# Running the FFN output of one sequence inside the attention stage of the next

## The chip, the cores and the metric

The kernel runs on all 8 cores of one Trainium2 chip. Each core computes 4 of the 32 sequences on its own; no core waits for another. The time is device microseconds (us) of the slowest core. The kernels have a second, slower state in some executions: the cores of one die, or of both, show a lower granted TensorE clock, and the time is 1% to 17% longer.

## The reference, cut to what matters

```python
h = rms_norm(x, g_pre_mix)
proj = h @ w_in                                    # 1024 -> 4352
o_a = stick_breaking_attention(q_a, k_a, v_a)      # 8 heads x 64, strictly causal
o_b = dilated windows, 3 groups x 4 heads x 64, rotary q/k, merged by denominators
o_c = softmax(q_c @ k_mem) @ v_mem                 # 4 heads x 128, 256 memory tokens
merged = sum(sigmoid(h @ w_gate + b)[j] * (o_j @ w_br_j) for j in (a, b, c))
x = x + rms_norm(merged @ w_o, g_post_mix)
h2 = rms_norm(x, g_pre_ffn)
f = (silu(h2 @ w_gate_ffn) * (h2 @ w_up)) @ w_ffn_out      # 1024 -> 2816 -> 1024
x = x + rms_norm(f, g_post_ffn)
```

x has the shape (32, 2048, 1024), in float32; the matmuls are bf16.

## The kernel before: the parts that matter

A recorder takes every operation with what it reads and writes. A list scheduler then walks through them with estimated durations and fixes the order on each engine, before anything runs. Operations belong to lanes; a lane spreads its operations over a range of virtual time, and the scheduler takes the ready one with the least virtual time. An operation that opens an accumulator also needs a free PSUM bank, out of the banks that its tile allows.

```python
LAT = {"pe": 230, "act": 130, "dve": 110, "pool": 130, "sp": 100}   # ns until another engine sees a result, as the plan estimates it
...
ALLB = tuple(range(8))
YB = (5, 6, 7)            # projections of both lanes, everything of the dilated and memory lane
# stick-breaking scores use the pairs (0,1) and (2,3), its output bank 4
...
for s in range(nseq):
    a0 = 2.0 * s
    ...
    xo = lane(a0 - 0.002, 1.0, lambda: lane_X(s, lastFI), True)    # stick-breaking
    yo = lane(a0, 1.0, lambda: lane_Y(s, lastFI), True)            # memory, then dilated
    if s == 0:
        lane(a0 + 0.01, 0.0, conv)      # f32 -> bf16 copies of the dense weights, DRAM to DRAM, by GpSimd
    def beta():                         # the dense stage
        M1(0, [lastX, lastY])           # gates and branch projections of 512 tokens
        for c in range(4):
            lm = M2(s, c)                       # output projection, norm, residual
            if c > 0: lo = [FO(s, c - 1)]       # FFN output: 4 blocks x 44 matmuls of 512 columns
            if c < 3: M1(c + 1, [lm])
            res["fi"] = FI(c, lo)               # FFN input
            if nxt: P1(s + 1, c, (1,), ALLB, [res["fi"]])   # next sequence's norm and transposes
        FO(s, 3)
    lane(a0 + 1.0, 1.0, beta, True)
```

In the stick-breaking lane the causal mask of a diagonal block is a matmul that adds a constant to the scores:

```python
mms.append((scores of head e, Kb, Q[:, e, lo:512], True, False))
if j >= 0:
    mms.append((first 128 columns of them, ident, negmaskA, False, False))
```

The softmax here doesn't subtract the row's maximum and nothing guards it: scores larger than these inputs give would overflow.

## Time and profile before

| | before |
|---|---|
| fast runs | 5693.09 and 5689.79 us |
| slow runs | 5913.08 us, later 6471.97 |
| core spans in the profiled run (fast) | 5657.5 to 5685.4 us |
| matmuls | 31176 |

I use one account through the whole document. From the trace I take every matmul's start, and subtract from each start-to-start distance the streaming time of the first of the two: columns / 2.4 + 2.5 ns. The two constants fit this trace: they give 55.8, 109.2, 162.5 and 215.8 ns for 128, 256, 384 and 512 columns, where the commonest distances are 56, 109, 162 and 216 ns, and the dense runs of the profile show 215.8 ns for 512. What is left is time in which TensorE didn't stream. Each matmul belongs to a stage by its place in the fixed order. On the profiled core the streaming sums to 5220.1 us, so what isn't streaming is 456 us of 5676. By stage, as the mean of the six cores whose traces miss no matmul:

| not streaming, us | seq 1 | seq 2 | seq 3 | seq 4 |
|---|---|---|---|---|
| attention stage (the first with the start-up) | 135.8 | 78.1 | 79.0 | 78.1 |
| dense stage, with the seam before it | 21.7 | 19.8 | 17.2 | 13.1 |

So two kinds of hole exist: some 80 us in every attention stage, and a seam of about 20. The lines of the profile that carry this are in the prediction.

### The profile page before, as it was taken

The page shows a single profiled execution, that of the slowest core. Times are in us where ns is not written, and L with a number is a line of the kernel's source. Part 1 is how long each engine was busy: PE and PEld are TensorE (multiplying, and loading weights), DVE is VectorE, ACT ScalarE, POOL GpSimd, SP SyncE. Part 2 cuts the span into 40 slices and gives each one's busy share as a digit, 9 for nine tenths or more (in the row PEclk, how much of TensorE's full clock was granted, in tenths as well). Part 3 has the DMA queues.
Part 4 walks back from the last instruction along what each step waited for, and adds up shares of the span by engine and source line. Part 5 has one row for each costly group of instructions (what it writes and reads, how often), then busy time and mean ns, then how long its engine had stood idle before and what let it go on. Part 6 is the DMA issues. An engine that isn't in the chain of part 4 may idle for free.

```text
span 5685.4 us, 80515 instructions; the slowest of 8 cores (5657.5 to 5685.4 us)
## 1 busy us (share of the span) xinstructions
PE 5421.8 (95%) x31176; PEld 2701.1 (48%) x31176; DVE 2627.5 (46%) x3867; ACT 2827.9 (50%) x4063; POOL 546.9 (10%) x1185
## 2 busy tenths in 40 slices
PE   7998999999999989999999998999999999999999
PEld 4454444444445544444444554444444555444444
DVE  5455643333446654433344665443333556534332
ACT  6876732222588862222268785222227878522221
POOL 2111101001101110110111001011010101000000
PEclk9999999999999999999999999999999999999999
DMA  7553365545300125554531003555442101354443
GB/s 151 66 65 68 79 218 180 175 156 178 87 18 12 27 84 199 179 182 150 169 81 23 12 22 105 196 178 178 155 160 71 23 12 30 122 184 168 166 170 105
DMA packets 115646, 654.57 MB, mean 115 GB/s; under 512 B 13392, under 2 KB 13392, under 8 KB 65744
## 3 DMA queue, kind: packets, MB, share of 16 engines
q1 hardware_dynamic: 103760, 576.80, 29.6%
q0 software_dynamic: 11520, 72.62, 8.4%
q8 instruction: 263, 4.31, 0.3%
q14 instruction: 103, 0.84, 0.0%
HBM read 646.48 MB, written 95.42 MB: 130 GB/s over the span
## 4 chain that ended last, share of the span: by engine, by line
PE 84%; ACT 7%; DVE 3%; DMA 2%; issue 2%; POOL 2%; SPq 0%; POOLq 0%; ACTq 0%; DVEq 0%
PE ps L551 83%; ACT arena L567 7%; DVE arena L578 2%; DMA arena<-wallbf 1%; PE ps L560 1%; POOL arena L578 1%; DMA arena<-arena 1%; POOL arena L615 1%; DVE arena L583 1%; ACT arena L571 0%; POOL arena L613 0%; DMA arena<-x 0%; DVE arena L574 0%; DVE arena L586 0%; DVE arena L589 0%
## 5 line engine op out<-in xcount | busy, mean ns | idle before, releaser
L551 PE MATMUL ps<-arena 128*128 128x512 bf16 (+3 forms) x30088 | 5370.9, 338 | 195.5 <-ACT arena L567 80.9
L551 PEld LDWEIGHTS ps<-arena 128*128 128x128 bf16 x30088 | 2636.5, 101 | 2876.6 <-issue 474.8
L567 ACT ACTIVATE arena<-ps 128x1024 f32<-128x1024 f32 (+6 forms) x2336 | 1713.2, 769 | 1913.9 <-PE ps L551 1889.6
L578 DVE TENSOR_TENSOR arena<-arena 128x1024 bf16<-128x1024 bf16 (+7 forms) x1172 | 772.1, 661 | 368.5 <-ACT arena L567 343.3
L567 ACT ACTIVATE arena<-arena 128x1024 bf16<-128x1024 f32 (+4 forms) x904 | 805.2, 907 | 191.1 <-DVE arena L578 87.2
L578 DVE TENSOR_TENSOR arena<-arena,ps 128x512 bf16<-128x512 f32 (+1 forms) x480 | 380.2, 793 | 1004.8 <-PE ps L551 1004.2
L578 DVE TENSOR_TENSOR arena<-ps,arena 128x512 bf16<-128x512 f32 (+3 forms) x872 | 658.1, 770 | 268.5 <-PE ps L551 172.0
L567 ACT ACTIVATE arena<-ps,arena 128x512 f32<-128x512 f32 x384 | 263.1, 687 | 647.9 <-PE ps L551 647.2
L586 DVE SCALAR_TENSOR_TENSOR arena<-arena,ps 128x512 f32<-128x512 f32 x384 | 263.0, 687 | 444.0 <-PE ps L551 253.0
L574 DVE CAST arena<-ps 128x256 bf16<-128x256 f32 (+1 forms) x437 | 224.8, 515 | 324.7 <-PE ps L551 319.9
L586 DVE SCALAR_TENSOR_TENSOR arena<-ps,arena 128x1024 f32<-128x1024 f32 x128 | 164.1, 1282 | 374.4 <-POOL arena L615 374.0
L613 POOL TENSOR_SCALAR arena<-arena 128x1 f32<-128x1 f32 x264 | 71.6, 271 | 2501.9 <-ACT arena L567 2500.7
L578 POOL TENSOR_TENSOR arena<-arena 128x512 bf16<-128x512 bf16 (+3 forms) x172 | 179.1, 1042 | 648.1 <-ACT arena L567 591.1
L615 POOL TENSOR_TENSOR arena<-arena 128x1 f32<-128x1 f32 x264 | 158.3, 600 | 21.2
L560 PE MATMUL ps<-arena 128*128 128x128 bf16 x1088 | 86.1, 224 | 59.1 <-DVE arena L583 32.4
L583 DVE TENSOR_SCALAR arena<-arena 128x1024 bf16<-128x1024 f32 (+1 forms) x105 | 82.8, 789 | 81.4 <-POOL arena L615 78.1
L592 POOL DMA_DIRECT2D arena<-wall x52 | 29.7, 571 | 930.0 <-PE ps L551 928.3
L560 PEld LDWEIGHTS ps<-arena 128*128 128x128 bf16 x1088 | 70.1, 100 | 98.2 <-issue 82.5
L754 POOL COPY arena<-arena 128x256 bf16<-128x256 bf16 x115 | 51.2, 445 | 601.4 <-ACT arena L567 596.3
L571 ACT ACTIVATE arena<-ps 128x512 bf16<-128x512 f32 (+3 forms) x135 | 69.5, 515 | 49.3 <-PE ps L551 46.3
L583 DVE TENSOR_SCALAR arena<-ps 64x512 bf16<-64x512 f32 x96 | 65.9, 687 | 53.3 <-PE ps L551 50.6
L589 POOL MEMSET arena<- 128x1 f32 (+2 forms) x286 | 44.4, 180 | 369.7 <-PE ps L551 220.7
(13 smaller groups left out, 198.6 us busy)
## 6 DMA issues: line engine op xcount, KB each, us to landing
arena<-wallbf SPq DMA_DIRECT2D x208, 1024.0 KB, 4.9
arena<-wallbf SPq DMA_DIRECT2D x128, 1088.0 KB, 6.4
arena<-x SPq DMA_DIRECT2D x128, 512.0 KB, 5.8
out<-arena SPq DMA_DIRECT2D x128, 512.0 KB, 3.6
arena<-out SPq DMA_DIRECT2D x64, 512.0 KB, 4.9
arena<-wall POOLq DMA_DIRECT2D x40, 768.0 KB, 6.5
wallbf<-wall POOLq DMA_DIRECT2D x27, 1024.0 KB, 14.6
arena<-wallbf SPq DMA_DIRECT2D x4, 5632.0 KB, 23.3
```

The source lines that it names most:

```text
L551: return e.matmul(out(), lhsT=lhsT, rhs=rhs, start=start, stop=stop, skip_group_check=True)
L560: fns = [lambda e, o=o, i=i: e.transpose(o(), i, ident) for o, i in outs]
L567: return R.add([("act", cact(n), [lambda e: e.activation(out=lz(out), in_=lz(in_), func=func, **kw)])], r=r, w=w, fence=fence)
L571: return ("act", cact(n), [lambda e: e.activation(out=lz(out), in_=lz(in_), func=AF.Copy, **kw)])
L574: return ("dve", cdve(n, mode), [lambda e: e.tensor_copy(out=lz(out), in_=lz(in_))])
L578: return (eng, c, [lambda e: e.tensor_tensor(out=lz(out), in0=lz(in0), in1=lz(in1), op=op)])
L583: return (eng, c, [lambda e: e.tensor_scalar(out=lz(out), in0=lz(in0), scalar1=s1, scalar2=s2, op0=op0, **kw)])
L586: return ("dve", cdve(n, mode), [lambda e: e.scalar_tensor_tensor(out=lz(out), in0=lz(in0), scalar=s, in1=lz(in1), op0=op0, op1=op1)])
L589: return R.add([(eng, cpool(n) / 2 if eng == "pool" else cdve(n, "cp"), [lambda e: e.memset(ap, val)])], w=[ap])
L613: R.add([("pool", 200, [lambda e: e.tensor_scalar(out=v[:, 1:2], in0=v[:, 0:1], scalar1=1.0 / D, scalar2=eps, op0=ALU.mult, op1=ALU.add)]) ...
L615: R.add([("pool", 600, [lambda e: e.tensor_tensor(out=v[:, 2:3], in0=v[:, 1:2], in1=half, op=ALU.pow)])], r=[v[:, 1:2]], w=[v[:, 2:3]])
L754: ("pool", 500, [lambda e, o=sn[:, :, lo:lo + 128], i=SPt[:, :, lo:lo + 128]: e.tensor_copy(out=o, in_=i)])],
```

## The change

Intent: fill the holes of an attention stage with matmuls that don't depend on it. The FFN output of sequence s-1 is a long row of 512-wide matmuls that nothing in sequence s needs. For that the FFN activations (11.5 MB a sequence) go to DRAM and come back, SBUF is laid out anew, and the outputs of the three branches go through DRAM too. The order within a dense stage changes as well: the FFN input of 512 tokens now comes after the output projection of the next 512 (M2(c), FI(c-1), M1(c+1), where it was M2(c), M1(c+1), FI(c)). Besides, the mask becomes an add on VectorE, the rotary tables come in pieces as they are needed, weight buffers of the dense stage become four instead of three, and the weight conversion has four copies in flight instead of two (the scheduler's estimate of its rate goes from 150 to 130 bytes a ns).

```diff
 # what runs where
+def lane_F(s, banks, tbs, halves=(0, 1), load=True, after=()):
+    for h in halves:                      # half of the 1024 output columns at a time
+        ... load that half of w_ffn_out
+        for tb in tbs:                    # 128 tokens
+            T = Tile(banks)
+            ... load the activations from DRAM in two parts; 12 + 10 matmuls of 512
+            h == 0: square-sum, copy the raw half to DRAM;  h == 1: the norm of both halves, residual, store
-xo = lane(a0 - 0.002, 1.0, ...X)
-yo = lane(a0, 1.0, ...Y)
+xo = lane(a0 - 0.002, 1.0 * ..., ...X)
+yo = lane(a0, 0.9 * ..., ...Y)                        # the dilated lane ends earlier
+if s > 0:
+    f1: lane_F(s-1, YB, all 16 blocks, half 0); lane_F(s-1, YB, 12 blocks, half 1)
+    lane(a0 + 0.001, ..., f1)                         # filler inside attention
+    fo = lane(2*s + 1.0, 0.05, lane_F(s-1, ALLB, the last NF2 = 4 blocks, half 1))   # on the seam
 # dense stage of all but the last sequence: no FO
 # the mask
-mms.append((first 128 columns of the scores, ident, negmaskA, False, False))
+zd = both heads' first 128 columns in PSUM
+R.add([a_tt("dve", zd, zd, negmaskA for both heads, ALU.add, 256)])
 # branch outputs: two staging buffers a lane, then DRAM
-o = O[tc][:, 6 + h, :]
+o = A16(Y_OS + (u % 2) * 1024, 512)
+ospill(s, tc, 6 + h, o, f"yo{u % 2}")
 # FFN activations to DRAM, 512 pieces of 256 bytes a store, 88 stores a sequence
+DMA(ft_d[...][:, :, j, :], FT[:, j, :], ...)
 # stick-breaking projection weights: one buffer instead of two
-W = [A16(X_W[a], 3072) for a in range(2)]
+W = A16(X_W, 3072)
 # conversion
-... f"cv{k % 2}" ... if k < 2
+... f"cv{k % 4}" ... if k < 4
... (layout, last sequence, constants cut)
```

## The prediction

> **What bounds the kernel now.** I read the page's busy shares and its slices first, then the same 600 us of an attention stage and of a dense stage side by side, then the matmuls of both by width, then the chain that ended last where the two stages meet.
>
> ```profile
> span 5685.4 us, 80515 instructions; the slowest of 8 cores (5657.5 to 5685.4 us)
> PE 5421.8 (95%) x31176; PEld 2701.1 (48%) x31176; DVE 2627.5 (46%) x3867; ACT 2827.9 (50%) x4063; POOL 546.9 (10%) x1185
> ...
> PE   7998999999999989999999998999999999999999
> ...
> ACT  6876732222588862222268785222227878522221
> ```
>
> TensorE is busy nearly everywhere; ScalarE shows four attention stages (digits 5 to 8) and four dense stages (2). By busy time TensorE has only 5% left. That reading misleads, as the next two views show.
>
> ```profile
> 1500.00:2100.00 600.00, 568.16 (x3908) 310.13 (x3907) 334.87 (x572) 485.65 (x658) 56.71 (x75) 0.99 0.10 23
> 2200.00:2800.00 600.00, 593.33 (x2888) 273.78 (x2887) 229.25 (x279) 151.10 (x247) 50.43 (x148) 1.00 0.50 174
> ```
>
> Columns: PE, weight load, DVE, ACT and POOL busy, granted clock, DMA share, GB/s. First row: attention stage of the second sequence. Second: its dense stage. The matmuls of the two, by width:
>
> ```profile
> L551 PE MATMUL ps<-arena 128*128 128x512 bf16 x1759 | 420.3, 380 | 16.0 <-ACT arena L567 12.0 <-DVE arena L574 1.4 <-issue 0.5
> L551 PE MATMUL ps<-arena 128*128 128x128 bf16 x1740 | 145.8, 221 | 11.8 <-POOL arena L578 8.6 <-DVE arena L578 1.9 <-ACT arena L567 1.1
> L551 PE MATMUL ps<-arena 128*128 128x256 bf16 x293 | 73.7, 336 | 3.9 <-ACT arena L567 1.6 <-DVE arena L578 1.2 <-DVE arena L583 0.8
> L551 PE MATMUL ps<-arena 128*128 128x384 bf16 x116 | 32.9, 326 | 0.1
> ...
> L551 PE MATMUL ps<-arena 128*128 128x512 bf16 x2696 | 586.0, 379 | 0.0
> L560 PE MATMUL ps<-arena 128*128 128x128 bf16 x192 | 14.6, 219 | 6.7 <-ACT arena L571 6.7
> ```
>
> The first four rows are the attention stage, the last two the dense one. A row's mean of 380 ns is the length of one overlapped matmul, not its price. The price is in the chain, where a dense run stands alone:
>
> ```profile
> 2547.07 158.85 PE ps L551 x736
> ```
>
> 158.85/736 = 215.8 ns per 512 columns, 0.4215 ns a column. The attention rows hold 1759x512 + 1740x128 + 293x256 + 116x384 = 1,242,880 columns = 524 us of streaming in 600: 76 us are lost. The dense rows hold 1,404,928 columns = 592 us in 600: 8 us lost. So the kernel is bound by TensorE's stream, tightly in the dense stage (99%) and loosely in attention (87%). An attention stage is some 630 us long, so it loses about 80 us; in the first one I expect more. Where the stage ends, the chain shows the worst of it:
>
> ```profile
> 2092.10 1.05 PE ps L551 x5
> 2093.17 0.39 ACT arena L567
> ...
> 2093.63 0.68 POOL arena L578
> ...
> 2094.44 1.04 PE ps L551 x5
> ...
> 2104.26 10.53 PE ps L551 x48
> 2114.86 19.71 DMA arena<-wallbf
> ```
>
> The dilated lane runs alone there: five small matmuls, an exp, a mask on GpSimd, again five matmuls. From 2079.4 to 2104.3 the chain's TensorE pieces sum to 7.6 us, so about 17 us are waits, and then the first dense weights arrive late (TensorE is busy 34.3 of the 40 us from 2100 to 2140). In 2060 to 2100 the mean granted clock is 0.81.
>
> [...]
>
> **The change, part by part.**
>
> *Moved.* The FFN output of the first three sequences: 16 blocks x 44 matmuls of 512 = 704 x 215.8 ns = 152 us each. It leaves the dense stage and becomes a third lane of the next attention stage, except four half blocks (88 matmuls, 19 us) that are put on the seam where attention ends. The last sequence keeps it in its dense stage. No matmul is saved by this; what is gained is that it lies in the 80 us of holes. From the instruction order of the changed kernel, filler is some 15% of the matmul columns all along each later attention stage, in runs of one to eight matmuls, and the dilated lane now ends before the stick-breaking lane, so the tail shown above has filler and seam blocks in it.
>
> How much of a hole is filled I choose so, for one later stage: the tail and seam (about 23 us) shrink to 4; the start of the stage, about 10, to 6; the rest, about 47, splits into roughly 11 us in which 128-wide matmuls do not reach the streaming rate (estimate from the trace's start stamps), which filler cannot give back, and 36 us of short waits, of which I keep 13. Reason for keeping some: the order on TensorE is fixed before the run, so a wait on a matmul that comes later than the scheduler thought also holds up the filler behind it. Remaining 34 of 80, gain 46 us, times 3 = 138 us.
>
> *Removed.* Causal mask matmuls of the stick-breaking lane: 16 units x 4 diagonal blocks x 2 heads = 128 of width 128 per sequence, 128 x 128 x 0.4215 = 6.9 us; 4 sequences: 28 us of TensorE time. *Added* for it: 64 DVE adds of 256 columns in PSUM per sequence; the 256-column cast from PSUM takes 423 ns, so about 27 us of DVE, which has some 45% idle. On the lane's latency each adds half a microsecond or more between score and exp, hidden while other lanes have matmuls.
>
> *Added on other engines*, per later stage: 32 half-width squares at about 0.6 us and 16 copies at 0.7 on ACT or DVE, 32 multiplies at 0.7 and 16 adds of 1.2 on DVE: about 20 to 30 us ACT, 42 to 53 DVE. ACT goes from 486 in 600 to some 530 in 700. Neither binds.
>
> *Added DMA.* FFN activations: 11.5 MB out, twice in; branch outputs 5.2 MB out and in; half-done FFN output 4.2 MB out and in; rotary tables again per round. About 70 MB per later attention stage, against 23 GB/s used now: harmless. In the dense stage the activation spill is 88 stores per sequence of 512 pieces of 256 B.
>
> *First attention stage.* No filler. Minus 7 us of masks, perhaps minus 5 at its tail because the two lanes end closer, plus some diagonal latency: I take 5 beyond the masks.
>
> *Dense stages.* Already at 99%; FFN input now comes after the next merge, which leaves slack but little to gain: 0.
>
> Sum: 138 + 28 + 5 = 171 us; from 5690 (the two fast runs): **5520 us**, a ratio of 0.970.
>
> **Rivals.** *Static order wins nothing in the middle*: short waits stay as they are, only tail, seam, start and masks are gained: 3 x 23 + 28 = 97, so 5590, within 2%. [...] Against it: the dense stage shows that with ready work in the queue almost nothing is lost.
>
> *Banks.* The filler takes its accumulator from the three PSUM banks that the dilated lane and all projections share. In the built order one filler tile stays open over about 20 us of other matmuls, so one of three banks is nearly always gone and the lanes may turn latency-bound at two. A stage would then lose 30 us more: about 5610.
>
> *Small stores.* 135,168 pieces of 256 B over the run. The page's main queue spent 29.6% of 16 engines on 103,760 packets, 260 ns for 5.6 KB; at that rate per byte a piece costs 12 ns, 33 us of all engines per dense stage. The dense stage uses half of the DMA; shortened by 152 us and with the moved traffic gone it would be near 0.6. Even at four times the cost it comes to about 0.75; only near 100 ns a piece would weights come late. Then TensorE waits 30 us or more per stage, about 5610 too.
>
> *Better than I choose.* If all but the 11 us goes: another 3 x 23 = 69 us, 5450.
>
> *Small copies hit by traffic.* In the first stage the chain has a 128 KB copy inside SBUF, 2.3 us in the median, that took 16.88 us behind the weight conversion. More queued loads could make the ones in later stages slow; each holds ScalarE, and with it the other lane. Worth 5 to 10 us a stage.
>
> ```profile
> 465.33 16.88 DMA arena<-arena
> ```
>
> **Range and chances.** 5450 to 5600 holds the central case and most of the first rival. 2% off is about 5579: central and better lie clear of it, the three bad rivals lie beyond it. I give them 0.2 together, hardly any of that slower by over 2%, since TensorE's own work only falls.
>
> **What would show it.** Matmul count 512 lower. Later attention stages near 700 us, with under 40 us not streaming, no granted clock near 0.8 at their end; dense stages of the first three near 620 us with DMA share about 0.6; the first attention stage within 15 us of before. I am wrong if the later stages still lose 60 us or more with waits on ACT or on a bank's reader (order or banks), or if the dense stages show TensorE waiting for weights with a DMA share over 0.8 (small stores).

The prices of the added operations match the means of the profile before: ScalarE took 0.60 us for 128x512 out of PSUM, VectorE 0.69 for a copy or a multiply of 128x512 and 1.22 for a float32 add of 128x1024. In the stretch from 1500 to 2100 us TensorE waited 14.9 us for ScalarE (28 times), 8.6 for GpSimd (12) and 5.8 for VectorE (16), never longer than 1.3 us.

## The result, and the profile after

The changed kernel took 5561.61, 5550.74 and 5550.63 us in its fast runs (one slow run: 5748.32). Executions in which one die ran at a lower clock are left out of the means. The ratio to before is 0.9759, 95% interval 0.9731 to 0.9787: faster. A ratio here is the mean time of one kernel's fast runs over that of the other's of the same rounds, so it isn't quite the ratio of the medians. Seven more runs of the same kernel in other rounds gave three fast ones, 5554.32, 5552.21 and 5563.60, ratio 0.9753 (0.9737 to 0.9769; the record calls this repeat unclear against the limit of 2%). So by the means of the fast runs, 5691.4 and 5554.3, 137 us were gained where 171 were predicted.

The page of the changed kernel's slowest core; first the span and the busy shares, then TensorE and ScalarE in 40 slices:

```profile
span 5560.1 us, 82537 instructions; the slowest of 8 cores (5526.5 to 5560.1 us)
...
PE 5365.4 (96%) x30664; PEld 2677.9 (48%) x30664; DVE 2707.3 (49%) x4106; ACT 2872.0 (52%) x4224; POOL 568.5 (10%) x1281
...
PE   6899989999999999999999999999999999999999
...
ACT  5787742224876763232577765332277776432121
```

512 matmuls fewer (31176 to 30664), as the masks are gone. The busy share moves from 95% to 96%: this view hardly shows a change of 137 us. ScalarE's attention stages are longer (digits 5 to 8) and its dense stages shorter.

The same pair of stretches as before: an attention stage of the second sequence and the dense stage after it (us, then busy time of TensorE, weight load, VectorE, ScalarE and GpSimd, granted clock, DMA share, GB/s):

```profile
1400.00:2000.00 600.00, 591.37 (x3932) 320.10 (x3931) 347.57 (x589) 442.35 (x630) 64.85 (x110) 1.00 0.35 99
2130.00:2600.00 470.00, 467.63 (x2306) 216.64 (x2305) 201.40 (x252) 142.20 (x226) 45.55 (x127) 1.00 0.70 224
```

And TensorE's matmuls of that attention stretch by width:

```profile
L581 PE MATMUL ps<-arena 128*128 128x512 bf16 x2023 | 480.0, 379 | 5.6 <-ACT arena L597 3.2 <-DVE arena L608 1.7
L581 PE MATMUL ps<-arena 128*128 128x128 bf16 x1560 | 122.1, 220 | 1.7 <-DVE arena L604 0.6 <-ACT arena L597 0.5 <-DVE arena L608 0.3
L581 PE MATMUL ps<-arena 128*128 128x256 bf16 x241 | 62.9, 329 | 1.3 <-ACT arena L597 0.7 <-DVE arena L608 0.2
L581 PE MATMUL ps<-arena 128*128 128x384 bf16 x108 | 29.6, 326 | 0.0
```

The columns are 2023x512 + 1560x128 + 241x256 + 108x384 = 1,338,624, at 0.4215 ns each 564 us of 600: 36 us lost. Before it was 524 of 600, in a stretch that held the last 20 us of the stage too. The idle column sums to 8.6 us only, since the bar of a 512-wide matmul is drawn 379 ns long and the next one may start after 216: a wait of less than 163 ns leaves no gap between bars. That is why the account goes by starts.

The account, as the mean of six cores in each of two fast runs (before: the table above):

| not streaming, us | seq 1 | seq 2 | seq 3 | seq 4 |
|---|---|---|---|---|
| attention stage, after | 160.6 | 48.4 | 48.5 | 48.9 |
| against before | +24.8 | -29.7 | -30.5 | -29.2 |
| dense stage, after | 4.3 | 6.6 | 5.9 | 11.4 |
| against before | -17.4 | -13.2 | -11.3 | -1.7 |

The streaming time fell by 28.6 us, 5220.1 to 5191.5. So 89.4 (three later attention stages) + 26.2 (dense stages 2 to 4 with their seams) + 17.4 (first dense stage with its seam) + 28.6 (masks) - 24.8 (first attention stage) = 136.8, which is the 137 us that the times show.

The two dense terms hide a gain that isn't the filler's. Take the first 60 us of a dense stage as its seam. Then the seams lost 9.6, 7.3, 5.1 and 3.8 us before and 0.8, 3.8, 2.9 and 4.4 after, and the rest of the dense stages 12.1, 12.5, 12.1 and 9.3 before and 4.0, 3.3, 3.3 and 7.2 after (means of the same cores). So of the 43.6 us some 14 came at the seams, 5 of them at the later three, and some 28 inside the dense stages (this cut leaves 1 us over). There the waits stood before the transposes that follow the output projection: 9.3 us a stage before, 1.2 to 1.8 after in the first three. In the dense stretch above they read as follows (TensorE's matmuls by width, from 2130 to 2600 us); the same row before, in 600 us, is in the prediction and has 6.7 us of idle time:

```profile
L590 PE MATMUL ps<-arena 128*128 128x128 bf16 x192 | 14.6, 219 | 0.6 <-ACT arena L601 0.6
```

The changed order of the dense stage gives TensorE other work at these points. That this order alone made the gain isn't shown, as no run restores the old one.

Where the later stages meet, the chain of waits (start us, us, what) now reads:

```profile
1999.38 36.01 PE ps L581 x171
...
2041.22 3.64 ACT arena L597 x6
...
2044.99 8.27 PE ps L581 x30
...
2054.36 12.05 DMA arena<-wallbf
```

The row of five small matmuls, an exp and a mask, again and again, is gone; 36 us of unbroken matmuls stand in its place. The end of the stage isn't closed, though. From 2035 to 2075 us TensorE waits 5.8 us for ScalarE and 4.2 us for the first dense weights. These still arrive late, with the DMA 0.92 busy from 2040 to 2080 us; for the rest of the 12 us that they take, filler blocks run.

In the first attention stage, which has no filler, the chain shows something that before didn't have:

```profile
102.96 33.26 DMA oall<-arena
...
136.92 0.69 DVE arena L604
137.74 10.65 PE ps L581 x56
...
174.09 18.47 DMA oall<-arena
...
239.79 13.21 DMA arena<-cf
```

128 KB stores of the memory branch's output take 33 and 18 us, and the load of a rotary table 13, while the weight conversion goes on. The waits of TensorE there (line, what it waited for: us in total, times, longest), first after, then before:

```profile
PE ps L581 <- ACT arena L597: 41.2, 39, 9.7
PE ps L581 <- DVE arena L604: 20.0, 5, 16.0
```

```profile
PE ps L551 <- ACT arena L567: 32.7, 27, 11.7
...
PE ps L551 <- DVE arena L574: 2.9, 4, 1.0
```

The cast that empties an accumulator (L604 after, L574 before) held TensorE for 20 us instead of 3, and the cast stood in VectorE's row behind an operation that waited for such a store (VectorE waited 29.6 us for these stores from 95 to 260 us, 17.0 the longest).

The spills themselves, from the lists of DMA issues (KB each, median us to landing), the queue and the mask on the page:

```profile
q1 hardware_dynamic: 341504, 788.15, 44.2%
...
L608 DVE TENSOR_TENSOR ps<-ps,arena 128x256 f32<-128x256 f32 x256 | 106.0, 427 | 55.1 <-PE ps L581 53.4
...
arena<-ftall SPq DMA_DIRECT2D x96, 384.0 KB, 3.8
ftall<-arena SPq DMA_DIRECT2D x264, 128.0 KB, 5.7
```

264 stores of 512 pieces are the 135,168 pieces of 256 B. They took 18 ns each in the trace (mean of all its packets of 256 B: 18.07 ns), the main queue's share of the DMA went from 29.6% to 44.2%, and the dense stage had 0.70 of the DMA busy with TensorE at 467.63 of 470 us.

### The profile page after: what moved, and what is told of

Same layout as the page of the kernel before. It is cut to its first block, busy times and chain, and to the rows that moved or that the text cites.

```text
span 5560.1 us, 82537 instructions; the slowest of 8 cores (5526.5 to 5560.1 us)
## 1 busy us (share of the span) xinstructions
PE 5365.4 (96%) x30664; PEld 2677.9 (48%) x30664; DVE 2707.3 (49%) x4106; ACT 2872.0 (52%) x4224; POOL 568.5 (10%) x1281
## 3 DMA queue, kind: packets, MB, share of 16 engines
q1 hardware_dynamic: 341504, 788.15, 44.2%
## 4 chain that ended last, share of the span: by engine, by line
PE 87%; ACT 5%; DMA 4%; DVE 2%; issue 1%; POOL 1%; SPq 0%; POOLq 0%; ACTq 0%; DVEq 0%
PE ps L581 86%; ACT arena L597 4%; DVE arena L608 2%; PE ps L590 1%; DMA arena<-wallbf 1%; DMA oall<-arena 1%; DMA arena<-arena 1%; DMA arena<-x 1%; ACT arena L601 0%; POOL arena L645 0%; SPq L622 0%; DVE arena L616 0%; DMA arena<-cf 0%; POOL arena L643 0%; DVE arena L604 0%
## 5 line engine op out<-in xcount | busy, mean ns | idle before, releaser
L581 PE MATMUL ps<-arena 128*128 128x512 bf16 (+3 forms) x29576 | 5317.5, 341 | 148.6 <-ACT arena L597 71.6
L597 ACT ACTIVATE arena<-ps 128x512 f32<-128x512 f32 (+6 forms) x2384 | 1725.3, 759 | 1765.8 <-PE ps L581 1675.8
L608 DVE TENSOR_TENSOR arena<-ps,arena 128x512 bf16<-128x512 f32 (+2 forms) x872 | 657.2, 769 | 279.2 <-PE ps L581 146.8
L604 DVE CAST arena<-ps 128x256 bf16<-128x256 f32 (+1 forms) x410 | 210.9, 516 | 264.3 <-PE ps L581 258.7
L616 DVE SCALAR_TENSOR_TENSOR arena<-ps,arena 128x1024 f32<-128x1024 f32 (+1 forms) x128 | 138.5, 1082 | 298.7 <-POOL arena L645 298.0
L608 POOL TENSOR_TENSOR arena<-arena 128x256 bf16<-128x256 bf16 (+3 forms) x211 | 212.6, 1009 | 506.3 <-ACT arena L597 490.0
L601 ACT ACTIVATE arena<-ps 128x256 bf16<-128x256 f32 (+3 forms) x196 | 101.5, 521 | 103.4 <-PE ps L581 99.3
L608 DVE TENSOR_TENSOR ps<-ps,arena 128x256 f32<-128x256 f32 x256 | 106.0, 427 | 55.1 <-PE ps L581 53.4
L619 POOL MEMSET arena<- 128x1 f32 (+3 forms) x286 | 40.1, 161 | 446.3 <-PE ps L581 214.2
```

The source lines that it names most:

```text
L581: return e.matmul(out(), lhsT=lhsT, rhs=rhs, start=start, stop=stop, skip_group_check=True)
L597: return R.add([("act", cact(n), [lambda e: e.activation(out=lz(out), in_=lz(in_), func=func, **kw)])], r=r, w=w, fence=fence)
L601: return ("act", cact(n), [lambda e: e.activation(out=lz(out), in_=lz(in_), func=AF.Copy, **kw)])
L604: return ("dve", cdve(n, mode), [lambda e: e.tensor_copy(out=lz(out), in_=lz(in_))])
L608: return (eng, c, [lambda e: e.tensor_tensor(out=lz(out), in0=lz(in0), in1=lz(in1), op=op)])
L616: return ("dve", cdve(n, mode), [lambda e: e.scalar_tensor_tensor(out=lz(out), in0=lz(in0), scalar=s, in1=lz(in1), op0=op0, op1=op1)])
```

## The experiments

All kernels gave a correct result. Times are of fast runs, against the changed kernel's 5550 to 5564. "Excess" is time not streaming; means are over the cores with full records. Some texts count the first stage another way (138 us where the account here has 160.6), so compare their differences, not their levels.

### 1. The four copies in flight

The changed kernel converts weights with four copies at once; if they delay the small stores, two should help.

```diff
-... f"cv{k % 4}" ... if k < 4
+... f"cv{k % 2}" ... if k < 2
```

> Changed kernel, but the weight conversion keeps two copies in flight instead of four, as before. Theory A (the first attention stage loses 36 us against my step because four conversion copies fill the DMA engines and the new branch-output stores queue behind them, the worst 33 us): the wait of 16 us at the start of the first stage shrinks to under 6, that stage's time not streaming falls from 138 us to 110 to 125, the whole to about 5530 to 5540. Theory B (what costs is the store staging of two buffers and the short rotary tables themselves, whatever the conversion does): first stage stays within 6 us of 138. Later stages the same in both.

Measured: 5555.62 and 5557.44 us. First attention stage 164.2 us (changed kernel: 160.6). Nothing gained: the number of copies alone isn't the cause.

### 2. All the FFN output on the seam

```diff
-lane(a0 + 0.001, ..., f1)
-fo = lane(2*s + 1.0 - F2B, 0.05, lane_F(s-1, ALLB, range(12, 16), (1,), False, [lastX]))
+fo = lane(2*s + 1.0 - F2B, 0.01, lane_F(s-1, ALLB, range(16), (0, 1), True, [lastX, lastY]))
```

> Changed kernel, but no filler inside attention: the whole FFN output of the previous sequence runs densely on the seam between attention and dense stage, on all banks. Everything else (spills, order of the dense stage, masks) stays. Theory A (the gain comes from filling holes): each later attention stage loses 75 to 90 us again instead of 47, so about 5630 to 5690, near the kernel before. Rival (the gain comes from the order of the dense stage, the masks and the seam): within 25 us of the changed kernel.

Measured: 5807.62, 5813.39 and 5824.40 us, so 260 slower. The later attention stages lose 94 us again instead of 48.6, and the dense stages with the FFN output in front 46, 45 and 53. One core's window of 160 us around a seam, same columns as above, has the DMA 0.83 busy and TensorE idle for 20 us:

```profile
2040.00:2200.00 160.00, 140.28 (x641) 62.73 (x639) 57.00 (x71) 23.05 (x50) 14.53 (x49) 0.96 0.83 267
```

So interleaving is worth some 45 us a stage, and the new structure without its filler is some 15 us a stage worse than before (94 against 78). The gain of 30 is the difference. (Where attention ends and the seam begins is partly a choice here: cut at the first matmul of the dense stage, the two losses are 89 and 51 to 58, and the worth of interleaving is 40.) All three fast runs have a lower granted clock, 0.976 to 0.981 where the changed kernel has 0.990 to 0.994; this is part of the 260 us.

### 3. The mask back on TensorE

```diff
+mms.append((first 128 columns of the scores, ident, negmaskA, False, False))
-R.add([a_tt("dve", zd, zd, negmaskA, ALU.add, 256)])
```

> Changed kernel with the causal mask back on TensorE (128 matmuls of width 128 per sequence) and no DVE adds. If my term is right, TensorE streams 28.6 us more and the total is 20 to 30 us longer. Rival (the DVE add between score and exp lengthens the lane where it is latency-bound, so in the first stage it costs what it saves): the first stage's lost time falls by 7 us or more, the later ones stay at 47, and the total is only 10 to 20 us longer.

Measured: 5580.53 and 5580.88 us, 26 slower. Streaming is 28.6 us longer; the later attention stages lose 45.9 instead of 48.6, the first 157.0 instead of 160.6. The masks are worth what their columns say. The add in PSUM costs nothing that can be seen: the 3 us that a later attention stage gains are lost again at the seam (dense stages 2 and 3 lose 11 instead of 6 to 7), and attention and dense stages 2 to 4 together lose 171 us in this run and 170 in the changed kernel.

### 4. No filler on the seam, and twice as much

```diff
-NF2 = 4
+NF2 = 0        # e4;   8 in e8
```

> Changed kernel with no half blocks kept for the seam: all filler runs inside attention. Theory (seam blocks cover the gap at the start of the dense stage): the dense stages of sequences 2 to 4 lose about 22 us again instead of 10 to 15, and the attention stages gain 0 to 8 by the extra filler: total 5 to 35 us longer than the changed kernel. Rival (the gap was covered by ending the dilated lane earlier, the seam blocks do nothing): within 5 us.

Measured: one fast run, 5622.13 us, 68 slower. The attention stages lose 54 and the dense stages 21, 20 and 29. The window at the seam shows what the four half blocks did: without them TensorE stands still for 25 of 80 us and loses granted clock; the changed kernel's stretch is under it.

```profile
2060.00:2140.00 80.00, 55.35 (x240) 23.52 (x239) 30.87 (x45) 28.59 (x41) 3.47 (x9) 0.83 0.61 196
```

```profile
2040.00:2120.00 80.00, 70.77 (x307) 31.05 (x308) 39.05 (x53) 27.64 (x44) 8.03 (x22) 0.91 0.84 265
```

> Changed kernel with eight half blocks kept for the seam instead of four. Removing the four cost 66 us in all (dense stages 40, attention 19, rest the clock), so the seam blocks are worth more than their 19 us of work. If that trend goes on: dense stages lose 5 to 8 us each instead of 10, attention stays within 3 of 47, total 5 to 15 us shorter. Rival (four already cover the gap, and more only leave holes in attention): attention stages lose 50 or more, total the same or up to 15 us longer.

Measured: 5587.60 and 5582.94 us. Attention loses 52 to 53, the dense stages 12, 12 and 23. What goes to the seam is missing inside the stage, so of 0, 4 and 8 four is the best.

### 5. More staging buffers for the memory branch

If TensorE waits because an output can't be staged while an older store crawls, six buffers instead of two take the wait away.

```diff
-o = A16(Y_OS + (u % 2) * 1024, 512)
+o = A16((six places)[u % 6], 512)
```

> Changed kernel; the memory branch's outputs wait for their store in six buffers instead of two (four of them lie in a rotary table buffer that is not yet in use). Theory A2 (the first stage's loss is in part VectorE standing behind output stores that lie 20 to 30 us in the DMA queues behind the weight conversion; two in flight instead of four gained only 4 us, so the depth of the conversion is not it, the depth of the staging is): from 130 to 200 us the time not streaming falls from 29 us to 10 to 15, and the first stage from 138 to 115 to 125. Rival (the stores only expose a wait that the next element, projection or rotary table, has anyway): first stage stays above 132. Later stages unchanged, as they show no wait on these stores.

Measured: 5564.60 and 5562.92 us, and a third fast run of 5591.97; first stage 163.8. The wait moved. The chain of that kernel, in the same place:

```profile
126.31 35.70 DMA arena<-wall
```

The stick-breaking lane's weights for the next heads, which have one buffer instead of two since the change, now arrive late behind the same conversion. The four further places are those of the second rotary-table buffer, and the later stages lost 51.5 us, 3 more than before the edit.

### 6. The conversion later

```diff
-after=arrived[15:16] if k < 4        # after the first inputs
+after=memdone[15:16] if k < 4        # after the memory branch
 # and in the plan: rate of the conversion 240 bytes a ns instead of 130
```

> Changed kernel; the weight conversion starts only when the memory branch of the first sequence has written its last output, everything else as in the changed kernel. Theory A2 (stores and conversion collide): the wait on stores goes, from 130 to 200 us under 15 us are lost instead of 29. What remains of the first stage: it may come back later as waits for rotary tables or the SBUF copies. Total 5 to 20 us shorter, unless the dense stage now waits for converted weights, which would show as lost time in the first dense stage above 10 us. Rival (stores are slow in the first stage whatever runs beside them): no change from 130 to 200 us.

Measured: 5601.04 and 5604.18 us. On the slowest core the excess from 130 to 200 us fell from 28.7 to 10.0, and from 200 to 300 it rose from 13 to 60.5 (over the cores with full records from 14 to 30 down to 9 to 10, and from 8 to 14 up to 49 to 61). The waits of VectorE between 200 and 400 us, and the longest piece of the chain:

```profile
DVE arena L608 <- DMA arena<-cf: 73.5, 6, 24.0
```

```profile
222.16 49.00 DMA arena<-cf
```

It is the rotary tables now, which come just in time since the change. In each of these runs another small load or store lay behind the conversion and waited; moving the conversion picked another victim.

### 7. The dilated lane ends later in the first sequence

```diff
-yo = lane(a0, YSPAN * ...)
+yo = lane(a0, (YSPAN if s else 0.95) * ...)
```

> Changed kernel; only in the first sequence the dilated lane is spread over 0.95 of the stage instead of 0.9, so that by instruction order both lanes end within 16 matmuls of each other instead of 68. Theory (without filler the stick-breaking lane is left alone at the end of the first stage and waits on ScalarE): the last part of the stage, from 670 us to the first dense matmul, loses 14 to 22 us instead of 31, total 8 to 17 us shorter. Rival (what is lost there is the copy inside SBUF that both need): within 5 us of 31.

Measured: one fast run, 5585.14 us. The profile fell in the slow state; on the undisturbed die (cores 5 to 7) the first dense stage lost 26 to 32 us instead of 4. The tail, from 670 us to the first dense matmul, lost 17 to 22 us where the changed kernel lost 20 to 31, so a few us were gained there. Then the first dense matmul waited 20 to 26 us for its weights: their load is issued only when the dilated lane has let its buffers go (on core 6 at 704 us and after, where the changed kernel issues the first at 661 to 682 us, by core, at 673 on core 6). So the early end of the dilated lane pays at the seam.

### 8. The conversion ahead of everything, in both kernels

A diagnosis, not a candidate: all copies are done before the first input is loaded, so nothing collides with them.

```diff
-DMA(wbf_d[...], wall_d[...], after=arrived[15:16] if k < 4 else [])
+DMA(wbf_d[...], wall_d[...], after=[])      # and all inputs wait for the last of them
```

> A diagnostic, slower on purpose: the whole weight conversion runs before anything else, so that no conversion runs beside the first attention stage. The total grows by the conversion, 250 to 450 us. Theory A3 (the first stage loses more than before because three new just-in-time transfers, output stores, the single weight buffer of the stick-breaking lane and the rotary tables, each meet the conversion): counted from its first projection, the first attention stage loses 75 to 95 us, no single wait over 5 us in its first two thirds, against about 138 with the start included and 100 without. Rival A4 (the stage's structure without filler, with the mask on VectorE and shared buffers, costs it): it still loses 115 or more.

> The mirror of the run that converts all weights first, with the kernel before: slower by 250 to 400 us on purpose. Without conversion beside it, the changed kernel's first stage with its start lost 113 us (initial wait for the conversion taken off) against a mean of 161 with it. If the kernel before suffers less from the conversion, as its branch outputs and rotary tables stay in SBUF, its first stage, a mean of 136, falls by only 15 to 30 us, to 106 to 121. If it suffers as much, it falls by 40 or more to below 96, and the first stage's loss in the changed kernel is its structure and not the collision.

Measured: one fast run each, 5802.39 us (changed) and 5956.00 us (before). Less the later start of the first matmul (some 290 us in both), the first attention stage lost 116 us in the changed kernel and 109 in before, means of three cores, against 160.6 and 135.8 with the conversion beside it. The collision costs 45 us after and 27 before; the new structure itself 7. Of the 24.8 us that the first stage lost, 18 are the collision. (Counted from the first matmul, six cores lost 102 to 105 us and 96 to 98. The first run by itself fell between its two theories; only the pair decides.)

### 9. Staging buffers and two copies together, and one step further

```diff
 # e10: the edits of experiments 5 and 1 together
 # e11: e10, and w_ffn_out is converted within the first dense stage
-while o < TOT:
+while o < OFF_FO:
 ...
+if s == 0 and c < 4: convert two pieces after each FFN input
```

> Six staging buffers for the memory branch and two conversion copies in flight together. Alone, each gained 1 to 4 us: with six buffers TensorE then stood 18 us before a weight load that lay 36 us behind four conversion copies in the same queue. If the two waits stand in a row (A3), both together give more than the sum: from 130 to 200 us under 18 us are lost instead of 29, first stage 120 to 130 instead of 138. If not (a common cause, as the bandwidth): 132 or more.

Measured: 5555.38 and 5551.66 us. The first stage lost 151.0 instead of 160.6, the later ones 51.5 instead of 48.6: 10 gained, 9 given back.

> As the run with six staging buffers and two copies in flight, and the last fifth of the conversion (the FFN output weights, which the changed kernel needs only one stage later) moves into the first dense stage. Theory: the end of the first attention stage no longer has conversion copies beside its SBUF copies and first weight loads, so from 600 us to the first dense matmul 10 to 20 us less are lost, and the first dense stage, with its DMA at 0.7, loses under 4 us more: 5525 to 5540. Rival: GpSimd's waits in the dense stage or the DMA there take it back: 5545 or more.

Measured: 5588.34 to 5596.31 us, ratio 0.9817 (0.9803 to 0.9830). The first stage fell to 146, but the first dense stage lost 37 to 56 us instead of 4. GpSimd's instructions have one order too, fixed by the program, and norms stand behind the copies in it. The copies wait for TensorE, and TensorE's transposes then wait for the norms. Waits between 800 and 1340 us of GpSimd, then of TensorE:

```profile
POOL wallbf L622 <- PE ps L590: 195.8, 3, 67.9
```

```profile
PE ps L590 <- DVE arena L613: 44.4, 3, 19.3
```

> The changed kernel once more, on the same chip and in the same rounds as its variants: 5550 to 5560 in the fast state, lost time per later attention stage within 2 us of 47. It is the reference for the others.

This is the changed kernel itself, for the fast runs named above (5554.32, 5552.21, 5563.60). Its six full cores lost 158.1 us in the first stage, 48.2, 48.7 and 48.9 later. So differences of 3 us a stage can be read, and of 10 in the first.

> A candidate to beat the changed kernel: two conversion copies in flight, and the six staging buffers in the first sequence alone, because with six in all sequences the later stages lost 51 us instead of 48. Means over the cores: first stage 148 to 155 instead of 161, later stages 47 to 50; total 5540 to 5552 where the changed kernel has 5552 to 5564.

Six buffers in the first sequence only, with two copies. All eleven runs were slow (5625.71 the lowest), so there is no time to compare. On the undisturbed die (cores 1 to 3) the later stages are at 48.3, so the 3 us of the six buffers in all sequences were the rotary-table buffer. But the first lost 160.5, no gain. From 100 to 200 us the excess is 12 instead of 26, as meant; from 200 to 300 it is 18 instead of 11, and the rest comes back at the end of the stage. A miss: the delay moved once more.

### 10. Filler in long runs

The built order has filler in runs of one to eight matmuls, and a filler accumulator stays open for 20 us. If an open accumulator is what starves the lanes, longer runs that close it after 8.5 us help. If fine mixing is what fills holes, they harm.

```diff
-PE([...], r=..., w=[T], after=after)
+PE([...], r=..., w=[T], after=after, grain=1e9)
```

> Changed kernel with the filler in uninterrupted runs of 10 to 12 matmuls (2.2 and 2.6 us) instead of one to eight: a filler tile then stays open over about 8.5 us of other matmuls instead of 20, so the third bank of the shared three is free most of the time. Bank theory (the filler's bank is what leaves 26 us of short waits in the middle of a later stage): those fall below 20 and the stage's lost time below 42. Order theory (matmuls that come later than planned hold up the filler behind them, whatever the banks; and longer runs delay the lanes): 26 or more in the middle, 47 or more in all, total the same or up to 30 us longer.

Measured: 5559.59 and 5561.88 us, ratio 0.9758. The profile fell in the slow state on die 0; on die 1 the later attention stages lost 52.8 instead of 48.6 (15 instead of 10 in the last 40 us, the middle within 2 us of the changed kernel's), and the dense stages 2 to 5 us less. So a shorter open time doesn't help. It doesn't say that banks don't matter, as the next group shows.

### 11. Banks and the plan

By then one question was left: why 48 us (52 with the seam, as the prediction counts) and not the predicted 34. The order is fixed by the scheduler, and the scheduler's own start times are a plan. I read the idle time of TensorE out of the plan of each kernel, and asked at each idle moment whether a matmul was ready and only its bank taken. In a later attention stage before: 56.7 us planned idle, 45.6 of them for want of a bank. After: 24.9, of them 22.0. (The text on record counts without the first operations of a stage, 52 for before.) In the middle of a stage all of the planned idle time is for want of a bank; in the last 40 us that holds for 1.1 of 12.2 us before and for 6.6 of 9.5 after. The 7 us for which the plan then waits for the first dense weights are not counted here. These numbers are the program's estimates, no measurement; three kernels put them to the test.

```diff
 # e16: the stick-breaking projections may take any of seven banks
+XB = (0, 1, 2, 3, 5, 6, 7)
-T = Tile(YB)
+T = Tile(banks)             # XB for these projections, YB for all others
 # e17: the shared pool has two banks
-YB = (5, 6, 7)
+YB = (6, 7)
 # e18: the plan takes results to be visible 100 ns later
-LAT = {"pe": 230, "act": 130, "dve": 110, "pool": 130, "sp": 100}
+LAT = {"pe": 330, "act": 230, "dve": 210, "pool": 230, "sp": 100}
```

> The projections of the stick-breaking lane (three accumulators a unit) may also take a free bank of the score pairs, seven banks in all instead of the three shared with the dilated lane and the filler. The program fixes TensorE's order ahead of the run, with estimated durations; in that plan a later attention stage of the changed kernel has 22.0 us of idle time, all of it moments in which a ready matmul finds no free bank, and here 15.7 us (before: 52). The dense stages' planned idle goes from 11.6 to 20.6. Bank theory (what is left in the middle is lack of a bank, and the chip adds a fixed 26 us to the plan, as 48 - 22 and 78 - 52 say): later attention stages 42 us (40 to 44), dense stages 4 to 9 us worse, the whole within 15 us of the changed kernel. Order theory (what is left is the chip straying from the plan): attention 47 to 51.

> Two banks instead of three for the dilated lane, the projections and the filler. Planned idle in a later attention stage 80 us instead of 22, all for want of a bank. Bank theory with a fixed 26 us on top: 106 us (95 to 115) not streaming in each later attention stage, against 48. If the plan's idle is not what the chip loses, or the filler's matmuls that are ready elsewhere cover it: under 75. Time some 200 us longer, first stage 25 to 35 us worse.

> Nothing but the order changes: the plan takes every result to be visible to another engine 100 ns later (330 instead of 230 ns from TensorE, 230 instead of 130 from ScalarE, 210 instead of 110 from VectorE). If the 26 us that the chip adds to the plan come from results that arrive later than planned, and hold up the matmuls behind them in the fixed order, a more cautious order loses less: attention 43 or lower although its planned idle is 23.5 instead of 22.0. If they come from matmuls that are themselves slower than the plan says (128-wide ones, ends of groups), attention stays at 48 to 51.

Measured:

| | time, fast | later attention stages, us not streaming | dense stages 2 to 4 |
|---|---|---|---|
| changed kernel | 5550 to 5564 | 48.4, 48.5, 48.9 | 6.6, 5.9, 11.4 |
| seven banks for the projections | 5557.71 (and 5569.20) | 43.5, 41.7, 43.7 | 13.2, 13.9, 12.8 |
| two banks | 5796.82 | 112.3, 112.4, 112.9 | 15.6, 15.3, 11.8 |
| plan with 100 ns more | 5515.11 | 38.8, 38.2, 41.2 | 4.6, 4.6, 9.1 |

(Means of six cores. In the columns of dense stages the seam is in.) All three came out as the bank theory and the late-result theory said. But seven banks gave back at the seam what they gained in attention, so they gained no time. TensorE's matmuls by width in 600 us of the two-bank kernel's stage:

```profile
L581 PE MATMUL ps<-arena 128*128 128x512 bf16 x1848 | 439.6, 380 | 26.5 <-DVE arena L608 10.1 <-ACT arena L597 8.9 <-ACT arena L601 4.0
L581 PE MATMUL ps<-arena 128*128 128x128 bf16 x1388 | 103.7, 221 | 6.7 <-DVE arena L608 2.7 <-ACT arena L597 1.6 <-DVE arena L604 1.1
L581 PE MATMUL ps<-arena 128*128 128x256 bf16 x230 | 59.5, 329 | 11.2 <-DVE arena L608 4.2 <-DVE arena L604 3.6 <-ACT arena L597 2.6
```

With one bank less the same filler is there, the same engines, and the idle column goes from 8.6 to 44 us: in this program the filler can't take a hole without an accumulator. The rows put 39 of these 44 us down to VectorE and ScalarE; in the program a bank goes to the next tile when one of them has read it. By the account that is 64 us a stage for one bank.

Split by part of the stage, planned idle against measured (matmuls that lose under 120 ns are kept apart as "small"; the plan has none of these):

| us | small | start, plan / chip | middle, plan / chip | last 40 us, plan / chip |
|---|---|---|---|---|
| before | 10.6 | 6.7 / 6.9 | 37.8 / 45.5 | 12.2 / 15.2 |
| changed kernel | 9.8 | 1.1 / 1.5 | 14.3 / 26.0 | 9.5 / 11.1 |
| seven banks | 11.2 | 0.4 / 0.3 | 11.8 / 24.3 | 11.7 / 8.8 |
| two banks | 12.3 | 2.6 / 2.7 | 75.4 / 83.8 | 18.0 / 14.9 |
| plan with 100 ns more | 8.9 | 0.5 / 0.0 | 19.0 / 23.4 | 7.8 / 6.9 |

The chip follows the plan closely. What it adds in the middle is 7.7 us before, 11.7 after, and 4.4 where the plan assumed later results. So a part of the losses is that results come later than planned, and the fixed order makes filler wait behind them; the more cautious order pays 4.7 us of planned idle in the middle and gets 7.3 back there, and 4 at the end of the stage. Two things stay untested. One value and one fast run don't exclude an order that is better by chance. And the same numbers also set when the plan takes a bank to be free again, so the edit isn't of late results alone.

The page of this last kernel's slowest core:

```profile
span 5513.6 us, 82623 instructions; the slowest of 8 cores (5487.0 to 5513.6 us)
...
PE 5336.0 (97%) x30664; PEld 2682.9 (49%) x30664; DVE 2689.3 (49%) x4092; ACT 2885.0 (52%) x4231; POOL 591.2 (11%) x1288
```

It is a version that beats both kernels: every one of its cores (5487 to 5514) ends ahead of every core of the changed kernel (5526 to 5560). The ratio is 5515.11 / 5694.74 = 0.968, with one fast run on each side; its other two runs and the other runs of before were slow, so there is no interval. Of the 39 us against the changed kernel, 28 lie in the later attention stages and 8 in the dense ones.

## Why the prediction was right or wrong

**The direction and the range held**: faster, 5554 (mean of the fast runs) in 5450 to 5600. The centre, 5520, was 34 us too low, and this is the sum of errors that partly cancel: 43 too much for the later stages with their seams, 29 too much for the first attention stage, 28 too little for the dense stages, 9 too little for the first seam. That the number came so near is in part luck. By its own steps:

*Masks, 28 us.* 28.6 measured in streaming. Right. The add on VectorE took 427 ns each, as the cast had suggested, and experiment 3 finds no cost in latency.

*Later stages with seams, 80 to 34, three times 46 = 138.* This is the term that failed. It measured 95: 89.4 in the attention stages and 5 at the seams. By parts of a stage: the 11 us of matmuls that don't reach the streaming rate stayed (9.8), and the start went to 1.5 where 6 was kept, better than thought. The step that failed most is "the tail and seam (about 23 us) shrink to 4", with its reason that filler and seam blocks lie there. The last 40 us went from 15.2 to 11.1 and the seam from 5.4 to 3.7 (means of three stages), a gain of 6 instead of 19. What the runs show in its place: near the end TensorE stands 5.4 us before a matmul that ScalarE releases, where the plan has 5.9 us for want of a bank, and then 4.2 us for the first dense weights. Of the 11.1 us, 9.5 were in the plan. The second step is "36 us of short waits, of which I keep 13". There were 45.5 to begin with and 26 stayed, so the gain was 19.5 where 23 was forecast. Its reason named only the fixed order's late results. Those are real (the plan with 100 ns more gains 28 us over the three stages), but the larger part, 14 of 26, is in the plan already, all of it for want of a bank.

*Dense stages, 0.* They gained some 28 us without their seams, most of it at the waits before the transposes. The step that failed is "Already at 99%; FFN input now comes after the next merge, which leaves slack but little to gain": 8 us lost of 600 are some 10 us in a stage, and most of them went. DMA share was 0.70 where 0.6 was predicted, and in the stretch shown TensorE waited for no weights.

*Banks* stood among the rivals, and was right in kind and wrong in size. It said that filler takes one bank of three and that a stage would lose 30 us more. Most of the plan's idle time is for want of a bank in both kernels (45.6 of 56.7 us before, 22.0 of 24.9 after), and taking a bank away costs 64 us a stage, but with three banks the filler still gained more than it took.

*The static order wins nothing in the middle* fell: the middle went from 45.5 to 26.

*First attention stage, +5 beyond the masks.* It lost 24.8 us, while the seam after it gained 9. Both follow from parts of the change that the prediction listed under "harmless" or didn't price there. Staging buffers, rotary tables and a weight buffer that is single now make the lanes depend on small transfers just in time, and in this stage they lie behind the weight conversion: 18 of the 25 us by experiment 8. The prediction had this mechanism ("small copies hit by traffic"), but placed it in the later stages. And the dilated lane's early end, named for the later tails, let the dense weights be loaded before the first seam.

*Small stores.* The rival fell. A piece of 256 B took 18 ns instead of 12, so 50% more than in proportion to its bytes, far from the 100 ns at which the prediction saw weights come late.

*The signs.* Of the signs that the prediction named, the matmul count and the length of the dense stages (616 to 623 us) came true; the later attention stages were 731 us long with 48 not streaming, the granted clock still fell to 0.83 in 40 us at their end, and the first one was 16 to 28 us longer than before. Filler is a fifth of the matmul columns of a later stage, not 15%.

What stays open: how much of the dense stages' gain is their new order; why the collision in the first stage moves rather than shrinks under each repair, beyond the victims that the experiments name; and how much more than 100 ns the plan should assume.

## What to carry to other kernels

Filler paid here where it could have its own accumulator at the moment of the hole (one bank less cost 64 us a stage): count the banks that are free there before counting the matmuls that could be moved. When the order is fixed ahead of the run, read its planned idle time next to the measured one; here 22.0 of the 24.9 us planned idle were for want of a bank, and against the part that wasn't planned more cautious latencies helped: a change of four numbers gave 39 us (one fast run). Keep a line in the account for every part of a change, also for those that were priced at nothing: here one of them hid 28 us. Buffers that were loaded long ahead and become just-in-time must be checked in the stage with the heaviest background transfer, not in the typical one (here they cost 18 us in the first stage).

## What the runs showed of the hardware

- Stores in pieces of 256 B took 18 ns each, against 12 by their bytes at the main queue's rate before (260 ns for 5.6 KB). 135,168 of them fitted in dense stages at 0.70 DMA share with TensorE busy 467.63 of 470 us.
- While the conversion from DRAM to DRAM went on in GpSimd's queue, 128 KB stores took 33 and 18 us (changed kernel), a 768 KB load 36 (experiment 5) and rotary tables of 256 KB up to 49 (experiment 6). The medians of these transfers over the whole run of the changed kernel are 2.0, 7.9 and 3.5 us.
- The fast runs of the changed kernel had all eight cores at work, at a mean granted clock of 0.990 to 0.994 over the whole 5.5 ms. In slow runs the clock of a die fell, as in these windows of a core of experiment 10 (first a dense stretch, 0.81, then one of the same core at full clock):

```profile
5400.00:5600.00 200.00, 197.80 (x768) 83.56 (x782) 59.45 (x75) 40.80 (x65) 7.84 (x20) 0.81 0.39 132
700.00:1300.00 600.00, 589.22 (x2840) 273.32 (x2898) 249.34 (x319) 185.97 (x289) 54.50 (x144) 1.00 0.71 222
```

- Interleaved work took banks of its own: 48.6 us were lost in a later attention stage with three shared banks and 112 with two.
- With an order that is fixed before the run against estimated latencies, 100 ns more in the estimate gave 39 us, in one fast run.
